# Fourteen tiles of the merge gates between the keys and the delta rule, parked in DRAM, and the recurrence traced ahead of the next projections

## The chip, the cores and the metric

The kernel runs on one core of a Trainium2 chip. The metric is the device time of one execution in microseconds, the median of several runs. The core has TensorE (PE: matmuls, and PEld: its weight loads), VectorE (DVE), ScalarE (ACT), GpSimd (POOL) and the queue engine SyncE (SP), which only issues DMAs here. Each engine carries out its instructions in a fixed order.

## The reference, cut to what matters

One decoder layer over 512 tokens of 1024 channels, in float32. The first sub-layer is a token mixer: one input projection `h @ w_in`, whose columns are shared out among two branches and the merge gates.

```python
h = x * (1 + sc1) + sh1                       # modulation, from c @ w_ada + b_ada
(q_att, c_kv, q_idx, k_idx, w_idx, qkv, a, b, z, gates) = split(h @ w_in)
y_att = dsa_attention(...)                    # top-128 keys a query, chosen by an indexer
y_dn  = gated_deltanet(...)                   # 8 heads, causal conv, delta rule in chunks, gated norm with z
gates = sigmoid(gates);  g_att, g_dn = gates[..., :1024], gates[..., 1024:]
merged = g_att * (y_att @ w_br_att) + g_dn * (y_dn @ w_br_dn)
x = layer_norm(alpha * x + (1 + gt1) * (merged @ w_out))
```

The second sub-layer is a mixture of 32 experts (two for each token), followed by a second layer norm. The gates depend on `h` and `w_in` alone, and are not used before the merge.

## The kernel before, in words

All activations are kept transposed, 128 channels by 512 tokens in a tile. A projection tile (`project`, L274) makes 128 output channels: 8 slices of the inner dimension, and for each slice 3 matmuls, since every float32 operand is split into a high and a low part (`mm3`, L226), so 24 matmuls of 512 columns. Its weights are a 128x1024 piece. Two pieces are loaded together into one of the three buffers "w" (`raw_of`, L242), and each is then split (`split_w`, L213) by ACT (high part, L222) and by VectorE or GpSimd (low part, L223). Which of the two takes the low part is told by the list `lo_eng`: GpSimd at first, VectorE for seven splits from the latent key/value tiles on (L501), then GpSimd again, and VectorE from the merge on (L861). The list `plan` (L232 to L240) holds the order of all weight pieces; `look_ahead` splits the next of them after each projection.

The stages, in order: the modulation of `x`; the small tile and the eight key tiles with their convolutions and norms (`key_norms`); the decays and the triangular matrices of the delta rule, whose 32x32 blocks are inverted on VectorE (L489 to L498) and pass through DRAM; the latent key/value tiles (`T_CKV`), the indexer's queries (`T_QI`) and its scores; the eight heads of the delta rule; eight heads of attention; the merge; the output projection with layer norm and routing; the experts.

A head of the delta rule is written as: transposes, the q.k products, the chain F, FtB, FtW, FtFtW that puts the 128x128 inverse XT together from the blocks in BB, the norm of the head before (`gated`), the next head's query and value projections with their convolutions (`queries_values`), the projection of z (`gate_z`), and then the recurrence over four chunks (L705 to L726: pw, wv, pv, vn, po, pS, St), of which each step needs the one before. After heads 2, 3 and 4 VectorE selects the top keys (`select`, 32 passes each).

The merge runs over eight channel tiles `d`: two gate tiles (`T_G + 2d` and `T_G + 2d + 1`, tanh by ACT into `gth`), two branch tiles, VectorE's products and sum, and the halves of the result. The pieces of the modulation that are needed last (`mod_cols`, L200: load of 1 MB of `w_ada` into a buffer "w", two passes of VectorE and a short one) stand there, three for each of `d` = 1 to 5 and one for `d` = 6.

The program is traced in this order, and a planner then fixes each engine's order: an instruction that was traced earlier goes first among those that its model takes to be ready. So the matmuls of a projection and the steps of a chain lie interleaved on PE. `issue_after` keeps an instruction behind another one. DMAs that `ld` issues are in SP's queue, those of `s.dma_start` in ACT's, those of `g.dma_start` in POOL's.

## Time and profile before

| | |
|---|---|
| median of 3 runs | 1262.67 us (1258.73 to 1264.76) |
| the profiled execution | 1262.51 us, span 1260.5 us |
| PE busy | 1181.4 us, 94% |
| VectorE busy | 786.0 us, 62% |
| ACT busy | 434.2 us, 34% |
| GpSimd busy | 215.8 us, 17% |
| HBM read and written | 287.05 MB, 3.70 MB |

The busy time of an engine is the time in which an instruction of it runs. Matmuls overlap in the array, so a busy PE is not always one at its peak. The granted clock is the share of TensorE's full clock that the chip allowed in a stretch; it has two levels, 2.4 GHz (1.0) and 1.2 GHz (0.5). Idle time before an instruction is put down to what released it.

### The profile page before, as it was taken

The page shows a single profiled execution, that of the slowest core. Times are in us where ns is not written, and L with a number is a line of the kernel's source. Part 1 is how long each engine was busy: PE and PEld are TensorE (multiplying, and loading weights), DVE is VectorE, ACT ScalarE, POOL GpSimd, SP SyncE. Part 2 cuts the span into 40 slices and gives each one's busy share as a digit, 9 for nine tenths or more (in the row PEclk, how much of TensorE's full clock was granted, in tenths as well). Part 3 has the DMA queues.
Part 4 walks back from the last instruction along what each step waited for, and adds up shares of the span by engine and source line. Part 5 has one row for each costly group of instructions (what it writes and reads, how often), then busy time and mean ns, then how long its engine had stood idle before and what let it go on. Part 6 is the DMA issues. An engine that isn't in the chain of part 4 may idle for free. (4 is left out here: it accounts for less than half of the span.)

```text
span 1260.5 us, 16329 instructions
## 1 busy us (share of the span) xinstructions
PE 1181.4 (94%) x6062; PEld 805.4 (64%) x6062; DVE 786.0 (62%) x1709; ACT 434.2 (34%) x916; POOL 215.8 (17%) x181
## 2 busy tenths in 40 slices
PE   4978988998899999999999979999999999999996
PEld 2767766776677777778888866455445555555543
DVE  6797998598996556876745884734444342433256
ACT  3454643665555656432222232121111111111102
POOL 4332334233232321000013331000000000000002
PEclk8999998999999999999999999999999999999997
DMA  7614414221111112266635677779999999999992
GB/s 276 260 67 130 122 43 138 60 44 54 49 66 38 67 54 81 83 252 234 252 132 200 244 300 304 309 291 420 420 421 420 422 421 420 421 421 422 420 381 103
DMA packets 76115, 291.84 MB, mean 232 GB/s; under 512 B 19297, under 2 KB 31745, under 8 KB 51458
## 3 DMA queue, kind: packets, MB, share of 16 engines
q1 hardware_dynamic: 58994, 282.47, 57.2%
q10 hardware_dynamic: 16352, 6.16, 2.1%
q0 software_dynamic: 688, 2.15, 0.5%
q8 instruction: 49, 0.80, 0.3%
q14 instruction: 32, 0.26, 0.1%
HBM read 287.05 MB, written 3.70 MB: 231 GB/s over the span
## 5 line engine op out<-in xcount | busy, mean ns | idle before, releaser
L227 PE MATMUL pj<-h_hi,w_hi 128*128 128x512 f32 (+1 forms) x504 | 202.5, 408 | 15.7 <-ACT h_hi L322 10.8
L229 PE MATMUL pj<-h_hi,w_lo 128*128 128x512 f32 (+1 forms) x504 | 206.1, 410 | 4.7 <-POOL w_lo L223 4.7
L228 PE MATMUL pj<-h_lo,w_hi 128*128 128x512 f32 (+1 forms) x504 | 206.5, 410 | 0.0
L223 POOL TENSOR_TENSOR w_lo<-wr,w_hi 128x1024 fp32r<-128x1024 f32 x43 | 108.8, 2533 | 205.5 <-ACT w_hi L222 163.9
L222 ACT ACTIVATE w_hi<-wr 128x1024 fp32r<-128x1024 f32 x85 | 89.7, 1057 | 133.3 <-PE pj L228 86.7
L227 PEld LDWEIGHTS pj<-h_hi,w_hi 128*128 128x128 f32 x504 | 97.1, 193 | 37.7 <-ACT h_hi L322 13.2
L1270 PE MATMUL pwg<-wg,xg 128*64 128x512 f32 x512 | 115.2, 595 | 0.0
L1270 PE MATMUL pwu<-wu,xg 128*64 128x512 f32 x512 | 115.2, 592 | 0.0
L229 PEld LDWEIGHTS pj<-h_hi,w_lo 128*128 128x128 f32 x504 | 98.1, 195 | 24.2 <-POOL w_lo L223 6.6
L228 PEld LDWEIGHTS pj<-h_lo,w_hi 128*128 128x128 f32 x504 | 97.4, 193 | 18.4 <-DVE h_lo L323 0.8
L1282 PE MATMUL py<-wd,hbTs 128*64 128x512 f32 x480 | 106.3, 593 | 0.0
L1270 PEld LDWEIGHTS pwu<-wu,xg 128*64 128x64 f32 x512 | 46.7, 137 | 62.9 <-issue 60.6
L1194 DVE TENSOR_TENSOR acc<-acc,comb 128x512 f32<-128x512 f32 (+1 forms) x126 | 77.4, 668 | 11.6 <-PE comb L1185 6.6
L1192 POOL TENSOR_TENSOR acc<-acc,ad 128x256 f32<-128x256 f32 x6 | 4.6, 788 | 449.9 <-PE comb L1185 447.0
L1144 DVE SCALAR_TENSOR_TENSOR eth<-eth,pwg 128x512 f32<-128x512 f32 x16 | 11.0, 687 | 112.5 <-ACT eth L1143 112.5
L1282 PEld LDWEIGHTS py<-wd,hbTs 128*64 128x64 f32 x480 | 40.0, 137 | 62.9 <-issue 62.9
L1270 PEld LDWEIGHTS pwg<-wg,xg 128*64 128x64 f32 x512 | 36.8, 137 | 65.3 <-issue 62.2
L223 DVE TENSOR_TENSOR w_lo<-wr,w_hi 128x1024 fp32r<-128x1024 f32 x42 | 55.6, 1325 | 29.1 <-ACT w_hi L222 28.2
L356 DVE SCALAR_TENSOR_TENSOR cacc<-pad,convw,cacc 128x512 f32<-128x512 f32 x72 | 68.5, 956 | 6.2 <-ACT cacc L354 6.1
L1163 DVE SCALAR_TENSOR_TENSOR ys<-py,gsl,gt2r 128x512 f32<-128x512 f32 (+1 forms) x34 | 24.3, 718 | 69.5 <-PE py L1282 62.9
L1146 DVE SCALAR_TENSOR_TENSOR hb<-eth,pwu 128x512 f32<-128x512 f32 x16 | 17.2, 1077 | 74.2 <-PE pwu L1270 74.2
L964 ACT ACTIVATE xg<-gx,h2c 128x256 f32<-128x256 f32 x32 | 17.8, 564 | 127.0 <-PE gx L1206 119.3
(492 smaller groups left out, 2339.9 us busy)
## 6 DMA issues: line engine op xcount, KB each, us to landing
wg<-in_w_gate_dram SPq DMA_DIRECT2D x64, 1024.0 KB, 11.4
wu<-in_w_up_dram SPq DMA_DIRECT2D x64, 1024.0 KB, 15.3
wd<-in_w_down_dram SPq DMA_DIRECT2D x60, 1024.0 KB, 12.4
wr<-in_w_in_dram SPq DMA_DIRECT2D x31, 1024.0 KB, 5.0
wada<-in_w_ada_dram SPq DMA_DIRECT2D x23, 1024.0 KB, 5.4
wr<-in_w_br_dram SPq DMA_DIRECT2D x8, 1024.0 KB, 6.4
gr<-g_rows ACTq DMA_DIRECT2D x16, 256.0 KB, 4.8
wr<-in_w_out_dram SPq DMA_DIRECT2D x4, 1024.0 KB, 5.0
```

Of the source, the lines that this page charges most:

```text
L222: s.activation(hi, raw, AF.Copy)
L223: (lo_eng.pop() if len(lo_eng) > 1 else lo_eng[0]).tensor_tensor(lo, raw, hi.bitcast(F32), op=OP.subtract)
L227: pe.matmul(o, a[0], b[0], start=start, stop=False)
L228: pe.matmul(o, a[0], b[1], start=False, stop=False)
L229: pe.matmul(o, a[1], b[0], start=False, stop=stop)
L356: v.scalar_tensor_tensor(acc, pad[:, i:i + S], convw[:, ct, i:i + 1], acc, op0=OP.mult, op1=OP.add)
L964: x = s.activation(xg[:, j, :n], o[:, 0, :n], AF.Identity, bias=h2c[:, 1, 1, j:j + 1], scale=h2c[:, 1, 0, j:j + 1])
L1146: rows_done[0] = v.scalar_tensor_tensor(hb[:n], th[:n].rearrange("s (p j) -> s j p", j=4), 0.5, pu[:n].rearrange("s (p j) -> s j p", j=4), ...
L1163: v.scalar_tensor_tensor(ys[:n, :w], py, gs, gt2r[:n, c], op0=OP.mult, op1=OP.mult)
L1194: v.tensor_tensor(acc[:, t, c], acc[:, t, c], o[:, :w], op=OP.add)
L1270: done = pe.matmul(o[64 * x:64 * x + 64], xg[:, 4 * i + j, c0 + 64 * x:c0 + 64 * x + 64], ws[x][:, j * FF:(j + 1) * FF], start=(i == 0 and ...
L1282: pe.matmul(py[c][64 * x:64 * x + 64], hT[:, 2 * i + j, 64 * x:64 * x + 64], ws[x][:, j, 512 * c:512 * c + 512], start=(i == 0 and j == 0) ...
```

## The change

Fourteen of the sixteen gate tiles (all but the first and the last) are projected earlier, two at a time: two after the key norms, two after the latent key/value tiles, and two in each of the heads 1 to 5 of the delta rule, behind that head's recurrence and the next head's projections. Each goes through tanh on ACT into a buffer and is written to a DRAM tensor by ACT's queue; in the merge, SP's queue loads it back into `gth`. In each head the recurrence is traced ahead of the next head's query and value projections and of z. Of the sixteen pieces of the modulation, eight are traced in attention, one at the start of each head, and eight in the merge, two for each of `d` = 1 to 4.

```diff
--- before.py
+++ after.py
@@ -41,6 +41,7 @@
 OVER = 16
 ACC_AT = 4
 GATED_AT = 3
+GATES_AT = (1, 2, 3, 4, 5)
 SELECT_AT = (2, 3, 4)
 
 EARLY = ['w', 'w', 'w', 'xa', 'o0', 'o1', 'a0', 'k0', 'k1', 'm0', 'm1', 'm2', 'acc0', 'k2', 'k3', 'm3', 'h0', 'h1', 'acc1']
@@ -228,15 +229,24 @@
         pe.matmul(o, a[0], b[1], start=False, stop=False)
         pe.matmul(o, a[1], b[0], start=False, stop=stop)
 
+    def early_gates(n):
+
+        return [("w_in", T_G + 1 + 2 * n + i) for i in range(2)]
+
     raws, pending = {}, {}
-    plan = [("w_in", i) for i in range(T_QI + 4)]
-    plan += [("w_in", T_QVZ + i) for i in range(3 * H)]
+    plan = [("w_in", i) for i in range(T_CKV)] + early_gates(0)
+    plan += [("w_in", i) for i in range(T_CKV, T_CKV + 2)] + early_gates(1) + [("w_in", i) for i in range(T_QI, T_QI + 4)]
+    plan += [("w_in", T_QVZ + i) for i in range(2)]
+    for h in range(H):
+        plan += [("w_in", T_QVZ + 2 + 3 * h + i) for i in range(3 if h < H - 1 else 1)]
+        plan += early_gates(GATES_AT.index(h) + 2) if h in GATES_AT else []
     for h in range(H):
         if h in (0, 3):
             plan.append(("w_ukv", h // 3 * 2))
         plan.append(("w_in", T_QA + h))
     for d in range(KT):
-        plan += [("w_in", T_G + 2 * d), ("w_in", T_G + 2 * d + 1), ("w_br", 2 * d + 1), ("w_br", 2 * d)]
+        plan += [("w_in", T_G + 2 * d + b) for b in range(2) if not 0 < 2 * d + b < 2 * KT - 1]
+        plan += [("w_br", 2 * d + 1), ("w_br", 2 * d)]
     plan += [("w_out", k) for k in range(2)]
 
     def raw_of(key, pool_=None):
@@ -280,6 +290,16 @@
             mm3(o, (hi[:, k, :], lo[:, k, :]), (r[0][:, k, first:], r[1][:, k, first:]), k == 0, k == KT - 1)
         look_ahead()
         return o
+
+    gate_rows = dram.tile([2 * KT, P, S], F32, name="gate_rows")
+
+    def work_out_gates(n, pool_):
+
+        for _, i in early_gates(n):
+            o = project("w_in", i)
+            x = pool_.tile([P, S], F32, name="gst", bufs=2)
+            s.activation(x, o, AF.Tanh, scale=0.5)
+            s.dma_start(gate_rows[i - T_G], x)
 
     h_hi = Parts(bigtile("h_hi", F32R), bigtile("h_hi", F32R))
     h_lo = Parts(bigtile("h_lo", F32R), bigtile("h_lo", F32R))
@@ -448,6 +468,7 @@
     for h in range(HB, H):
         conv_silu(first.get(T_K + h) or project("w_in", T_K + h), 8 + h, kT[:, h, :])
     key_norms(1)
+    work_out_gates(0, ip)
 
     def decay(h, e=g):
 
@@ -505,6 +526,7 @@
         o = project("w_in", T_CKV + c)
         s.activation(sqc[:, c, :], o, AF.Square)
         v.tensor_scalar(cks[:, c, :], o, kvg[:, c:c + 1], None, op0=OP.mult)
+    work_out_gates(1, ip)
 
     p_ss = pc("p_ss", (P, NT))
     for t in range(NT):
@@ -689,14 +711,8 @@
         xt_done = v.tensor_tensor(XT[:64, :, 64:], XT[:64, :, 64:], four("FtFtW", F[:96, :, :64], FW[:96]), op=OP.add)
         if done:
             gated(*done)
-        if h < H - 1:
-            qv[h + 1] = queries_values(h + 1)
         if h == H - 1:
             late_rows.append(smalltile("ou"))
-        zs = gate_z(h)
-        if h == H - 1:
-            V.append([bigtile("V", F32R) for _ in range(2)])
-            att_values(0)
 
         po = pc("po", (P, NT, P))
         St = None
@@ -729,6 +745,14 @@
         else:
             ou = dq.tile([P, NT, P], F32, name="ou", bufs=1)
         s.activation(ou, po, AF.Copy)
+        if h < H - 1:
+            qv[h + 1] = queries_values(h + 1)
+        zs = gate_z(h)
+        if h == H - 1:
+            V.append([bigtile("V", F32R) for _ in range(2)])
+            att_values(0)
+        if h in GATES_AT:
+            work_out_gates(GATES_AT.index(h) + 2, dq)
         if h in SELECT_AT:
             with tc.issue_after(xt_done.ins):
                 select(1 + SELECT_AT.index(h))
@@ -748,6 +772,7 @@
         if h == 3:
             V.append([tp_.tile([P, NT, S], F32R, name=n) for n in ("V_hi", "V_lo")])
             att_values(1)
+        mod_cols(16 + 2 * h, tp_)
         V_hi, V_lo = V[h // 4]
         look_ahead()
         o = project("w_in", T_QA + h)
@@ -860,16 +885,18 @@
     ys = (Parts(ya_hi, yb[0]), Parts(*ya_lo, yb[1])), (Parts(*yd[0]), Parts(*yd[1]))
     lo_eng[0] = v
     for d in range(KT):
-        for j in range(16 + 6 * (d - 1), min(22 + 6 * (d - 1), 48), 2) if 1 <= d <= 6 else ():
+        for j in (28 + 4 * d, 30 + 4 * d) if 1 <= d <= 4 else ():
             mod_cols(j, ep)
         if d == KT - 2:
             m_rows = mod_rows()
             h2c = first_norm_rows()
         part = [None, None]
         for b in range(2):
-            o = project("w_in", T_G + 2 * d + b)
             part[b] = ep.tile([P, S], F32, name="gth", bufs=4)
-            s.activation(part[b], o, AF.Tanh, scale=0.5)
+            if 0 < 2 * d + b < 2 * KT - 1:
+                ld(part[b], gate_rows[2 * d + b])
+            else:
+                s.activation(part[b], project("w_in", T_G + 2 * d + b), AF.Tanh, scale=0.5)
         for b in (1, 0):
             o = project("w_br", 2 * d + b, rhs=ys[b])
             v.scalar_tensor_tensor(part[b], part[b], 1.0, o, op0=OP.add, op1=OP.mult)
```

## Rows read from the trace of the kernel before

**Rows 1.** Busy time of the engines by stretch; last: granted clock, DMA share, GB/s.
```profile
core 0: us, PE busy (x) PEld busy (x) DVE busy (x) ACT busy (x) POOL busy (x), PEclk, DMA share, GB/s
100.00:225.00 125.00, 110.13 (x555) 90.02 (x555) 104.57 (x224) 63.80 (x141) 43.17 (x54) 0.95 0.37 111
225.00:400.00 175.00, 157.97 (x972) 126.48 (x971) 147.50 (x388) 101.53 (x280) 54.20 (x32) 0.98 0.18 51
100.00:400.00 300.00, 268.10 (x1524) 216.50 (x1524) 252.07 (x611) 165.32 (x421) 97.37 (x86) 0.97 0.26 76
400.00:520.00 120.00, 119.24 (x618) 93.68 (x617) 73.88 (x253) 69.63 (x162) 26.64 (x16) 1.00 0.17 58
523.90:692.10 168.20, 168.20 (x723) 135.26 (x722) 109.42 (x174) 48.02 (x80) 17.99 (x17) 1.00 0.59 213
692.00:1260.00 568.00, 547.18 (x2889) 302.34 (x2887) 268.01 (x520) 102.73 (x178) 37.22 (x24) 0.98 0.90 365
```

**Rows 2.** The same view, 25 us in the heads with a selection.
```profile
350.00:375.00 25.00, 22.06 (x128) 17.62 (x126) 25.00 (x58) 13.21 (x37) 9.01 (x5) 1.00 0.13 43
```

**Rows 3.** PE's waits from 100 to 400 us: total, times, longest.
```profile
PE pw L706 <- DVE St L725: 5.5, 2, 3.8
PE pv L712 <- DVE wv L708: 5.4, 4, 1.8
...
PE pv L712 <- DVE XT L689: 2.3, 2, 1.5
PE vtr L643 <- DVE vT L359: 2.2, 1, 2.2
```

**Rows 4.** Waits of SP's queue from 690 to 900 us.
```profile
SPq L1107 <- PE po L229: 29.9, 6, 13.0
```

**Rows 5.** PE in order of time, about the start of the merge: start, us.
```profile
519.40 0.45 PE L228 MATMUL pj<-h_lo,w_hi 128*128 128x512 f32 x1
...
524.12 0.40 PE L227 MATMUL pj<-yd_hi,w_hi 128*128 128x512 f32 x1
```

**Rows 6.** The page's groups by line: count, busy us, mean ns, idle before.
```profile
L223 POOL TENSOR_TENSOR w_lo<-wr,w_hi 128x1024 fp32r<-128x1024 f32 x43 | 108.8, 2533 | 205.5 <-ACT w_hi L222 163.9
L222 ACT ACTIVATE w_hi<-wr 128x1024 fp32r<-128x1024 f32 x85 | 89.7, 1057 | 133.3 <-PE pj L228 86.7
...
L223 DVE TENSOR_TENSOR w_lo<-wr,w_hi 128x1024 fp32r<-128x1024 f32 x42 | 55.6, 1325 | 29.1 <-ACT w_hi L222 28.2
```

**Rows 7.** Instructions on the tile gth: ns shortest/median/longest, first and last start.
```profile
L880 DVE TENSOR_TENSOR m<-gth,m x32: 271/284/2500, 539.3 to 697.6; 128x128 fp32r<-128x128 f32 x32
L872 ACT ACTIVATE gth<-pj x16: 575/580/598, 520.1 to 681.9; 128x512 f32<-128x512 f32 x16
L875 DVE SCALAR_TENSOR_TENSOR gth<-gth,pj x16: 681/687/689, 530.9 to 692.3; 128x512 f32<-128x512 f32 x16
```

**Rows 8.** The same view of the tile gr.
```profile
L455 ACTq DMA_DIRECT2D gr<-g_rows x16: 366/382/726, 100.0 to 319.9; - x16
```

**Rows 9.** All engines in order of time, about 160 us.
```profile
159.80 0.74 DVE L552 SCALAR_TENSOR_TENSOR isc<-rl,widx,isc 128x512 f32<-128x512 f32 x1
...
160.45 2.63 POOL L223 TENSOR_TENSOR w_lo<-wr,w_hi 128x1024 fp32r<-128x1024 f32 x1 [7.30 <-ACT w_hi L222]
...
160.89 2.74 DVE L552 SCALAR_TENSOR_TENSOR isc<-rl,widx,isc 128x512 f32<-128x512 f32 x1
```

**Rows 10.** VectorE's groups by line from 523 to 692 us.
```profile
L205 DVE SCALAR_TENSOR_TENSOR junk<-wada,cond 128x1024 bf16<-128x1024 f32 x32 | 39.1, 1222 | 6.9 <-DMA wada<-in_w_ada_dram 6.2
...
L207 DVE SCALAR_TENSOR_TENSOR mod<-mod,bada 128x2 f32<-128x2 f32 x16 | 2.5, 157 | 0.3
```

**Rows 11.** The page's DMA issues: count, KB each, us to landing.
```profile
wada<-in_w_ada_dram SPq DMA_DIRECT2D x23, 1024.0 KB, 5.4
wr<-in_w_br_dram SPq DMA_DIRECT2D x8, 1024.0 KB, 6.4
gr<-g_rows ACTq DMA_DIRECT2D x16, 256.0 KB, 4.8
```

## The prediction

> **What bounds the kernel now.** I read the stretches first, because the page's 94% for PE is a mean over stages with different limits. In the merge, from 523.9 to 692.1 us, PE is busy for all 168.2 us [rows 1]: the reader is to see a stage with no hole in it, where the 30 tiles that run there (16 branch tiles, 14 gate tiles, each 24 matmuls) cost 168.2 / 30 = 5.61 us each, and where VectorE has 109.4 us of work and so room. From 100 to 400 us, which holds the end of the key work, the inverses, the index scores and the eight heads of the delta rule, PE is busy for 268.1 of 300 us, a share of 0.894; 31.9 us are idle, and its granted clock averages 0.97, against 1.00 in the merge [rows 1]. A mean of 0.97 over 300 us of the levels 2.4 and 1.2 GHz is 18 us at the lower one, so up to 9 us of PE's busy time there is slowness. VectorE is the other party: 252.1 of 300 us, and 25.00 of 25.00 us between 350 and 375 [rows 1, 2]. The list of waits then says what PE's idle time there is: short waits for VectorE's steps in the recurrence (St 5.5 us, wv 5.4, XT 2.3) and for the next head's values (vT 2.2) [rows 3]. So one stage is filled up by PE, and an earlier one has holes that no work fills, or that PE's fixed order cannot fill.
>
> After the merge DMA is busy for 0.90 of the time [rows 1], and SP's loads of expert weights wait for the products that free their buffers, 29.9 us of it for the output projection [rows 4]. What follows the merge therefore starts from its end, and I let it move as one block.
>
> **The change, part by part.**
> *Gates out of the merge.* After the change 16 branch tiles and the last gate tile stand there: 13 x 5.61 = 72.9 us go. The 14th, the second gate tile, is what PE runs from 519.40 until the first product with yd at 524.12 [rows 5]. Without it that product waits only for the halves of y; it could come at once (4.7 us more) or no earlier (0). I take 3.5, since the halves of eight heads are made one after the other just then. Sum: -76.4 us.
>
> *The same tiles from 100 to 400 us.* 14 x 5.61 = 78.5 us of PE work are added to a stretch with 31.9 us of holes, so its length is (268.1 + 78.5 - c) / u, where c is clock won back and u PE's busy share. The ends: u = 0.894 as now, and u = 119.2 / 120 = 0.994, which attention reaches in the same kernel with the next projection always at hand and VectorE at 73.9 of 120 us [rows 1]. The new stretch lies between: the gate tiles need no VectorE pass after their product, so VectorE's share falls, but PE still carries its instructions in one planned order, and a recurrence step at the head of it that VectorE delivers late stops the gate tile behind it too. I take 0.95, the middle rounded up, since four tiles fall in 100 to 225 us (PE 110.1 of 125) and ten in the heads. For c I take 4.5 of the 9 us (ends 0 and 9), since a denser PE leaves fewer idle spells. (346.6 - 4.5) / 0.95 = 360.1: the stretch grows by 60.1 us.
>
> The Trainium skill, in "Perfetto Trace Analysis", section "Identifying the Most-Contended Engine", holds that matmul busy time is a poor measure of PE's headroom and that the weight loads' busy share is a better one. By the rows that share is 216.5 / 300 = 0.722 here and 135.3 / 168.2 = 0.804 in the merge [rows 1]; with 14 x 135.3 / 30 = 63.1 us added and the merge's share the stretch would last 279.6 / 0.804 = 348 us and the kernel end near 1238. With attention's share, 93.7 / 120 = 0.781, it would last 358 us, close to the sum above.
>
> *What comes with a moved tile.* Each brings its split, on ACT 1.06 us and on POOL 2.53 instead of VectorE's 1.33 in the merge [rows 6], a tanh of 0.58 [rows 7] and a write to DRAM issued by ACT, nearest a row read's 0.38 [rows 8]. ACT gets 14 x (1.06 + 0.58 + 0.38) = 28 us on 165, over 360 us: about 54%, so nothing waits in the mean, and the cover is PE's own 5.6 us a tile. POOL gets 35 us on 97; queued behind a split are the next head's decay, qd and the clearing of BB, which can start up to 2.5 us later a head. The price of a POOL split for VectorE shows at 160.45: while it runs, a pass that took 0.74 us just before takes 2.74 [rows 9]. So 14 more cost VectorE 0 to 14 x 2.0 = 28 us; I take half, 14, with which VectorE is at 266 of 360 us. The mean is no bound, but the heads with a selection are close to one, and this is why u is not nearer to 0.994. SP gets no issue here beyond loads that it had later.
>
> *The recurrence ahead of the next projections.* The matmuls that this reorders all remain. At best the recurrence's three waits (5.5 + 5.4 + 2.3 = 13.2 us) go [rows 3]; at worst the next head's values come late every time, 7 x 2.2 = 15.4 us. PE already runs the two interleaved, so I take 0 beyond u.
>
> *Columns of the modulation in attention.* Eight of the sixteen pieces move there, each two passes of 1.222 us and one of 0.157 [rows 10]: 2.60 us, 20.8 in all on VectorE, 94.7 of 120 us. SP issues one load of 1 MB a head ahead of the next query tile's; three buffers hold it, the keys' weights and the query pair. PE's filler covers it; without cover, one pass late in each head, 8 x 1.22 = 9.8 us. I take +1.
>
> *The merge's new pace.* A channel tile lasts PE 2 x 5.61 = 11.2 us instead of 22.4. VectorE's work for one of tiles 1 to 4 is two splits (2 x 1.33), two products and a sum (3 x 0.69), four halves (4 x 0.28) [rows 6, 7] and two pieces (2 x 2.60): 11.1 us, level with PE. The loads are one branch pair and two pieces through three buffers: 6.4 + 5.4 + 5.4 = 17.2 us from issue to landing if each waited for the one before [rows 11], 6.0 too many in each of four tiles, 24 us; 0 if they overlap. SP also issues the 14 reads of parked gates, 256 KB each, for which 4.8 us is the nearest row [rows 11]; such a read waits for one of four buffers, and the next weight pair is queued behind it, but two channel tiles of lead cover that. I take +3.
>
> Sum: -76.4 + 60.1 + 1 + 3 = -12.3 us on the profiled execution's 1262.5 (span 1260.5 and 2.0 around it), so 1250. The median of the three runs is 1262.7, so no correction is needed.
>
> **The rivals.**
> *The holes all fill.* With u = 0.994 and the full 9 us of clock the stretch lasts 337.6 / 0.994 = 339.6, +39.6 us; with no stall elsewhere -36.8, so 1226. For it: gate tiles depend on nothing of the heads, and attention shows the share. Against it: VectorE's full slices and PE's short waits, which are not for lack of a filler alone. Chance 0.20.
>
> *PE's share does not rise.* Place: the heads with a selection. Price: 346.6 / 0.894 = 387.7, +87.7 us; with the rest -76.4 + 87.7 + 4 = +15.3, so 1278. It decides from a share below 342.1 / (300 + 72.4) = 0.919, where the stretch takes all that the merge gives. For it: every wait in the list is for VectorE or ACT, which get later when POOL splits more. Against it: a head that waits for VectorE is just where a free tile can run. Chance 0.13. The Trainium skill, in "SBUF — State Buffer", section "Who interferes with whom", speaks for this rival: a VectorE instruction with two SBUF inputs and a GpSimd one that reads SBUF exclude each other for a whole instruction. The trace agrees at 160.89 (2.74 for 0.74 us); by it all 14 splits would cost their whole 2.53 us, 35 us instead of 14.
>
> *The merge waits for its weights.* If three buffers make the loads follow one another, the merge pays 24 us and not 3: +8.7, so 1271. For it: the pace doubles while two pieces a tile remain. Against it: the pieces are not needed before the seventh tile and can slip into the tiles that have none. Chance 0.09.
>
> **How the numbers follow.** The forecast has 0.58, with an own range of 1239 (u = 0.97, no stall elsewhere) to 1258 (u = 0.93). The measurement tells 0.5%, 6.3 us, from no change: faster is below 1256.2, slower above 1268.8. Faster: 0.45 of the forecast's 0.58, most of its own range lying below 1256, and the 0.20 of filled holes, 0.65. Within: the rest of the forecast, 0.13. Slower: 0.13 + 0.09 = 0.22. The range goes from 1228, just above the end where all is filled, to 1272, past the weights' case.
>
> **What would show it.** Right: the stretch from the first product with yd to the output projection near 95 us after 168; the stretch up to attention about 60 us longer, PE at 0.95; POOL splits between 100 and 460 us 14 more; attention within 2 us. Wrong: PE's share there at 0.92 or less, or 0.98; holes of PE in the merge that end with a load or a VectorE split; VectorE busy above 290 us in the stretch; the expert phase not moved with the merge.

## The result: 2.3% slower, and the profile after

The changed kernel takes 1292.2 us (median of four runs, 1290.8 to 1295.7) where the kernel before took 1263.7 beside it: a ratio of 1.0234, with a 95% interval from 1.0207 to 1.0261. The forecast was 1250 us and its range ended at 1272. The profiled span is 1289.0 us, 28.5 us longer than before.

I cut both traces at the same events, because the borders of [rows 1] fall elsewhere in the changed kernel: the copy `ou` of the last head (end of the delta rule), the last copy of `oT` (end of attention) and the first product of the output projection (end of the merge).

| stretch | before | after | change | forecast |
|---|---|---|---|---|
| 100 us to the last `ou` copy | 314.4 | 393.9 | +79.5 | +60.1 |
| attention | 105.8 | 132.9 | +27.1 | +1 |
| merge | 172.0 | 98.7 | -73.3 | -76.4 + 3 |
| the rest | 568.3 | 563.6 | -4.7 | 0 |

The merge did what was forecast, to a tenth of a microsecond. The two stretches that had to take in what left it cost 45.5 us more than forecast. Here are the windows of the kernel after that answer to [rows 1] (columns as there); the first two are the part up to the first head's `ou` copy and the heads, the last is what follows the merge.

```profile
100.00:256.40 156.40, 131.41 (x682) 107.88 (x681) 114.56 (x245) 76.10 (x176) 42.97 (x57) 0.93 0.32 97
256.40:493.90 237.50, 224.63 (x1256) 177.73 (x1254) 163.75 (x398) 119.06 (x293) 84.32 (x45) 1.00 0.26 82
100.00:493.90 393.90, 356.04 (x1934) 285.60 (x1934) 278.31 (x642) 195.16 (x468) 127.29 (x101) 0.97 0.28 87
493.90:626.80 132.90, 117.85 (x560) 93.98 (x559) 98.61 (x272) 64.00 (x152) 28.15 (x16) 0.94 0.33 116
626.80:725.50 98.70, 95.47 (x407) 75.58 (x407) 76.09 (x126) 28.61 (x55) 18.11 (x17) 1.00 0.68 239
725.50:1289.00 563.50, 541.75 (x2888) 298.88 (x2886) 267.94 (x520) 102.67 (x178) 38.48 (x24) 0.99 0.90 367
```

The same borders in the kernel before:

```profile
100.00:239.20 139.20, 122.86 (x645) 100.60 (x645) 112.00 (x243) 71.32 (x169) 45.44 (x56) 0.95 0.34 101
239.20:414.40 175.20, 159.39 (x959) 126.90 (x957) 146.59 (x389) 100.91 (x268) 56.56 (x32) 0.98 0.19 53
100.00:414.40 314.40, 282.25 (x1602) 227.49 (x1601) 258.58 (x631) 172.23 (x436) 102.00 (x88) 0.97 0.25 74
414.40:520.20 105.80, 105.29 (x541) 82.85 (x540) 67.37 (x231) 62.92 (x150) 22.00 (x15) 1.00 0.18 60
```

The reader is to see three things. First, from 100 us to the end of the heads PE's share is 356.04 / 393.9 = 0.904; it was 0.898, the forecast needed 0.95, and below 0.919 the stretch takes all that the merge gives. Read as lengths: PE's busy time grew by 356.04 - 282.25 = 73.8 us, and its idle time did not shrink but grew, from 314.4 - 282.25 = 32.2 us to 37.9. On balance no hole was filled. Second, the two parts of that stretch differ. The heads did reach 0.946, and their idle time fell from 15.8 to 12.9 us; in the part before them the share fell from 0.883 to 0.840, the idle time rose from 16.3 to 25.0 us, and the granted clock fell from 0.95 to 0.93. Third, attention, where PE had been busy for 105.29 of 105.8 us, now has 15 us of holes and a clock of 0.94.

PE's waits in the kernel after say what ends those holes (in us: total, times, longest). First those from 100 to 494 us, then those of attention; in attention the kernel before has one wait, of 0.2 us.

```profile
PE pv L728 <- DVE wv L724: 8.8, 6, 1.9
PE pidx L566 <- ACT rl L569: 8.3, 4, 4.3
PE kk L496 <- DVE NTm L498: 7.5, 3, 5.6
PE vtr L665 <- DVE vT L379: 2.6, 1, 2.6
...
```

```profile
PE pt L815 <- DVE pr L812: 6.7, 4, 2.3
PE sc L229 <- DVE K_lo L797: 3.1, 1, 3.1
PE sc L229 <- DVE qk L797: 3.0, 1, 3.0
PE oT L228 <- ACT T_hi L816: 1.0, 2, 0.8
...
```

The waits for `NTm` (matrices of the delta rule) and for `rl` (index scores) stand in the part before the first `ou` copy. They were there before, about half as long; [rows 3] shows the lines around them:

```profile
PE kk L475 <- DVE NTm L477: 4.2, 2, 2.1
PE pidx L544 <- ACT rl L547: 3.4, 2, 1.8
```

That part holds one long chain: the products `kk`, the matrices `NTm`, their way through DRAM, the inversion of the blocks on VectorE, and the way back through `r_dram` to the first head. Here are the first of the inversion's two lines and the write behind it, in the kernel before and after (ns shortest/median/longest, first and last start in us):

```profile
L493 DVE TENSOR_TENSOR y<-y,y x31: 184/348/422, 146.1 to 207.8; 128x31 f32<-128x31 f32 x2, 128x60 f32<-128x60 f32 x2, 128x87 f32<-128x87 f32 x2, 128x112 f32<-128x112 f32 x2
...
L498 POOL DMA_DIRECT2D r_dram<-y x1: 577/577/577, 210.3 to 210.3; - x1
```

```profile
L514 DVE TENSOR_TENSOR y<-y,y x31: 180/357/2374, 158.9 to 218.8; 128x31 f32<-128x31 f32 x2, 128x60 f32<-128x60 f32 x2, 128x87 f32<-128x87 f32 x2, 128x112 f32<-128x112 f32 x2
...
L519 POOL DMA_DIRECT2D r_dram<-y x1: 577/577/577, 223.3 to 223.3; - x1
```

From the start of the inversion to the write it takes 64 us in both kernels. It starts 12.8 us later, and the write comes 13.0 us later: the chain was pushed back as a whole, and work that PE does ahead of it fills none of its holes. In ten_heads, which lacks the four gate tiles of this part, the inversion starts at 146.9 us and the write at 211.9.

`K_lo`, `qk` and `pr` are steps of attention's own chain on VectorE. Why they are late is seen in the kernel after in order of time at 549 us (start, us; in brackets the engine's idle time before it):

```profile
549.08 9.79 SPq L203 DMA_DIRECT2D wada<-in_w_ada_dram  x2
...
553.93 1.23 DVE L206 SCALAR_TENSOR_TENSOR junk<-wada,cond 128x1024 bf16<-128x1024 f32 x1 [5.77 <-DMA wada<-in_w_ada_dram]
...
554.19 3.20 POOL L224 TENSOR_TENSOR w_lo<-wr,w_hi 128x1024 fp32r<-128x1024 f32 x1 [5.13 <-ACT w_hi L223]
...
554.80 0.59 ACT L796 ACTIVATE K_hi<-pK 128x512 fp32r<-128x512 f32 x1
...
555.20 3.27 DVE L206 SCALAR_TENSOR_TENSOR junk<-wada,cond 128x1024 bf16<-128x1024 f32 x1
...
559.00 0.68 DVE L797 TENSOR_TENSOR K_lo<-pK,K_hi 128x512 fp32r<-128x512 f32 x1
```

VectorE stands idle for 5.77 us because the next pass in its order, a pass of the modulation, waits for its weights; then the first pass takes 1.23 us, the second, beside a GpSimd split, 3.27. `K_lo`, whose input `K_hi` was there at 554.80 + 0.59 = 555.4, starts at 559.00, and PE waits 3.1 us for it. Over the whole of attention, VectorE's groups by line (busy us, mean ns | idle before):

```profile
L206 DVE SCALAR_TENSOR_TENSOR junk<-wada,cond 128x1024 bf16<-128x1024 f32 x16 | 24.1, 1506 | 5.8 <-DMA wada<-in_w_ada_dram 5.8
...
L208 DVE SCALAR_TENSOR_TENSOR mod<-mod,bada 128x2 f32<-128x2 f32 x8 | 6.3, 787 | 0.0
```

So the pieces take 30.4 us there instead of the 20.8 of the forecast. The load is late once only; the smallest of a piece's three operations, 157 ns in the merge [rows 10], averages 787 and costs more. Five of its eight runs take 141 to 152 ns. The other three take 1.65 to 2.27 us, and each lies beside a GpSimd split, as here:

```profile
530.00 2.37 POOL L224 TENSOR_TENSOR w_lo<-wr,w_hi 128x1024 fp32r<-128x1024 f32 x1 [10.50 <-ACT w_hi L223]
...
530.12 2.27 DVE L208 SCALAR_TENSOR_TENSOR mod<-mod,bada 128x2 f32<-128x2 f32 x1
...
533.48 0.30 PE L815 MATMUL pt<-ident,pr 128*128 128x128 f32 x1 [2.28 <-DVE pr L812]
```

Behind each of the three, `pr` comes late and PE waits for it: 2.0, 2.3 and 1.6 us of the 6.7 in the list. The page's line of the splits answers to [rows 6]: of the 85 splits GpSimd now has 57, 14 more, and VectorE 14 fewer, since the gates' splits in the merge had been its own.

```profile
L224 POOL TENSOR_TENSOR w_lo<-wr,w_hi 128x1024 fp32r<-128x1024 f32 x57 | 141.9, 2490 | 297.1 <-ACT w_hi L223 241.9
```

### The profile page after: what moved, and what is told of

Read it like the earlier page. It is cut to its first block, busy times and chain, and to the rows that moved or that the text cites. A ratio compares the mean times of both kernels' runs of the same rounds, so it can differ in the third digit from the quotient of the medians.

```text
span 1289.0 us, 16416 instructions
## 1 busy us (share of the span) xinstructions
PE 1184.0 (92%) x6062; PEld 807.7 (63%) x6062; DVE 798.3 (62%) x1695; ACT 433.8 (34%) x916; POOL 250.4 (19%) x195
## 5 line engine op out<-in xcount | busy, mean ns | idle before, releaser
L228 PE MATMUL pj<-h_hi,w_hi 128*128 128x512 f32 (+1 forms) x504 | 204.9, 413 | 14.9 <-ACT h_hi L342 13.0
L224 POOL TENSOR_TENSOR w_lo<-wr,w_hi 128x1024 fp32r<-128x1024 f32 x57 | 141.9, 2490 | 297.1 <-ACT w_hi L223 241.9
L376 DVE SCALAR_TENSOR_TENSOR cacc<-pad,convw,cacc 128x512 f32<-128x512 f32 x72 | 77.0, 1074 | 8.4 <-ACT cacc L374 8.3
L991 ACT ACTIVATE xg<-gx,h2c 128x256 f32<-128x256 f32 x32 | 17.8, 564 | 127.0 <-PE gx L1233 119.3
L1212 PE MATMUL comb<-yh,places 128*128 128x512 f32 (+1 forms) x132 | 53.0, 405 | 0.5 <-ACT eth L1261 0.5
## 6 DMA issues: line engine op xcount, KB each, us to landing
wg<-in_w_gate_dram SPq DMA_DIRECT2D x64, 1024.0 KB, 11.3
wd<-in_w_down_dram SPq DMA_DIRECT2D x60, 1024.0 KB, 12.3
gr<-g_rows ACTq DMA_DIRECT2D x16, 256.0 KB, 5.1
```

Source lines behind the costliest of these rows:

```text
L224: (lo_eng.pop() if len(lo_eng) > 1 else lo_eng[0]).tensor_tensor(lo, raw, hi.bitcast(F32), op=OP.subtract)
L228: pe.matmul(o, a[0], b[0], start=start, stop=False)
L376: v.scalar_tensor_tensor(acc, pad[:, i:i + S], convw[:, ct, i:i + 1], acc, op0=OP.mult, op1=OP.add)
L991: x = s.activation(xg[:, j, :n], o[:, 0, :n], AF.Identity, bias=h2c[:, 1, 1, j:j + 1], scale=h2c[:, 1, 0, j:j + 1])
L1212: pe.matmul(o[:, :w], OT[:n, t * P:(t + 1) * P], y, start=(i == 0), stop=(not bias and i == len(parts) - 1))
```

## The experiments

Every kernel was timed in turn with the kernel before; ratios are to it, with 95% intervals. The table has the lengths in us of the four stretches named above in each profiled execution, and the start of the first `ou` copy; the sections follow it. Each length is that of one execution. What follows the merge is the same work in every run and yet lies between 563.6 and 575.1 us, so differences of a few us in a stretch are not to be leaned on.

| run | first ou | 100 to last ou | attention | merge | rest | ratio |
|---|---|---|---|---|---|---|
| before | 239.2 | 314.4 | 105.8 | 172.0 | 568.3 | 1 |
| after | 256.4 | 393.9 | 132.9 | 98.7 | 563.6 | 1.0234 |
| mod_alone | 243.0 | 319.5 | 115.4 | 171.3 | 569.0 | 1.0077 |
| rec_alone | 244.2 | 317.0 | 113.6 | 171.9 | 570.6 | 1.0056 |
| gates_alone | 259.5 | 408.9 | 107.2 | 116.6 | 570.6 | 1.0269 |
| mod_back | 256.1 | 395.4 | 111.2 | 112.8 | 570.0 | 1.0177 |
| gates_before_rec | 253.6 | 395.8 | 111.2 | 113.1 | 570.8 | 1.0201 |
| one_slice | 248.2 | 347.4 | 111.2 | 113.9 | 569.0 | 0.9865 |
| no_products | 239.8 | 311.3 | 111.4 | 111.9 | 566.2 | 0.9523 |
| four_early | 256.0 | 360.1 | 107.3 | 161.8 | 570.4 | 1.0274 |
| four_slice | 251.1 | 339.7 | 107.3 | 161.5 | 566.4 | 1.0072 |
| four_early_dve | 254.6 | 346.8 | 107.0 | 162.9 | 571.3 | 1.0172 |
| split_on_dve | 253.3 | 380.5 | 111.2 | 114.8 | 572.5 | 1.0092 |
| ten_heads | 244.1 | 359.6 | 111.2 | 119.3 | 570.4 | 1.0005 |
| ten_heads_dve | 241.2 | 353.9 | 111.2 | 120.7 | 575.1 | 0.9970 |
| spread14_dve | 230.2 | 374.7 | 114.2 | 112.1 | 568.5 | 1.0092 |
| ten_dve_norec | 240.8 | 356.7 | 107.2 | 118.8 | 571.2 | 0.9968 |

### One part of the change alone

mod_alone puts only the eight pieces of the modulation into attention, on the kernel before:

```diff
+        mod_cols(16 + 2 * h, tp_)                       # at the start of each head of attention
-        for j in range(16 + 6 * (d - 1), min(22 + 6 * (d - 1), 48), 2) if 1 <= d <= 6 else ():
+        for j in (28 + 4 * d, 30 + 4 * d) if 1 <= d <= 4 else ():
```

> The kernel before, with only the eight pieces of the modulation moved into attention. In the changed kernel the time from the last head's ou to the last oT copy grew from 105 to 132 us. Theory (the pieces' VectorE passes and their loads' waits stand in the softmax chain): attention about 125 to 132 us here too, the merge no shorter since PE fills it, the whole 1280 to 1290. Rival (attention grew since its filler, the gate tiles, is gone or since the selections slipped): attention within 3 us of 105, the whole 1261 to 1267.

Measured: 1273.2 us, 1.0077 [1.0055, 1.0099]. Attention is 9.6 us longer and the merge, which PE fills, is not shorter (-0.7). That lies between the two readings. PE's waits in attention add up to 6.2 us here against 14.9 in the kernel after; none of the eight sums of two columns is held (the longest takes 472 ns). The pieces alone are a small loss.

rec_alone traces only the recurrence ahead of the next head's projections (the block that calls `queries_values`, `gate_z` and `att_values` moves behind the `ou` copy).

> The kernel before, with only the recurrence traced ahead of the next projections. Theory (this reorders work that PE interleaves anyway): first to last ou within 6 us of the 175 before, the whole 1258 to 1270. Rival (this order makes the heads wait, and is what took the holes' filling away): first to last ou 185 to 200 us, the whole 1274 to 1289.

Measured: 1270.7 us, 1.0056 [1.0036, 1.0076]. The heads, from the first to the last `ou` copy, are 2.4 us shorter; the first `ou` copy comes 5.0 later and attention is 7.8 longer. Part of the 7.8 is the border: the last head's z and attention's first values now stand behind the `ou` copy that ends the heads, so 556 products lie in attention instead of 541, some 3.5 us at 5.61 / 24 each. The 5.0 go with the granted clock, which up to the first `ou` copy is 0.92 here and 0.95 in the kernel before.

gates_alone takes the fourteen gates out of the merge and leaves recurrence and pieces as before; mod_back is the kernel after with the sixteen pieces back in the merge (the diff of mod_alone the other way round).

> The kernel before, with only the fourteen gate tiles moved (the sixteen pieces of the modulation stay in the merge, the recurrence stays behind the projections). Theory (the gate tiles run as blocks between the heads, not in the holes): first ou at 255 and first to last ou 230 to 240 us, attention near 105, the merge a little longer than in the changed kernel because five tiles carry three pieces at 11.2 us; the whole 1268 to 1282. Rival (the recurrence order spoilt the filling): first to last ou 205 to 220 us, the whole 1240 to 1256.

> The changed kernel with the eight pieces of the modulation back in the merge. Theory (pieces in attention cost 27 us): attention near 105 us, the merge 8 to 15 us longer than 99, the whole 1270 to 1282. Rival (attention's growth has another cause): attention stays at 125 or more, the whole 1290 to 1305.

Measured: gates_alone 1300.4 us, 1.0269 [1.0205, 1.0333]; mod_back 1288.5 us, 1.0177 [1.0131, 1.0223]. Read as a ladder: the gates alone lengthen the stretch up to the last `ou` copy by 94.5 us and shorten the merge by 55.4; the recurrence ahead then gives 13.5 us back in that stretch and takes 4.0 in attention; the pieces in attention cost 21.7 us there and give the merge 14.1. So the recurrence ahead, a loss of 7 us by itself, is worth 12 us with the gates in the heads by the medians, though the two intervals overlap; the 4.0 us in attention are the border again (559 products for 538). The place of the pieces hardly moves the whole: the profiled spans are 1289.0 us after and 1289.3 in mod_back, and the intervals overlap. Both kernels came out slower than expected (1282 at most). PE's waits in the merge of mod_back show why the pieces matter there now:

```profile
PE pj L228 <- ACT w_hi L223: 6.2, 3, 2.8
PE pj L230 <- DVE w_lo L224: 5.3, 6, 1.6
PE pj L229 <- DVE yd_lo L768: 1.6, 3, 0.9
```

With the gates gone the merge is no longer full: PE is busy for 99.3 of 112.8 us, and what it waits for are splits, of weights and of the halves. One of the waits for `w_hi` goes back to a load. SP can issue it only when VectorE is through with a piece (661.37), ACT stands idle until it lands, and PE waits 2.27 us:

```profile
661.37 0.38 SPq L262 DMA_DIRECT2D wr<-in_w_br_dram  x1
...
669.10 1.06 ACT L223 ACTIVATE w_hi<-wr 128x1024 fp32r<-128x1024 f32 x1 [11.42 <-DMA wr<-in_w_br_dram]
...
670.21 0.51 PE L228 MATMUL pj<-yd_hi,w_hi 128*128 128x512 f32 x1 [2.27 <-ACT w_hi L223]
```

The forecast's 3 us for this merge holds with half of the pieces away, not with all sixteen in it.

gates_before_rec is mod_back with a head's two gate tiles traced and planned ahead of its recurrence and not behind it.

> The changed kernel with the pieces in the merge, in which a head's two gate tiles are traced and planned right after XT and ahead of the recurrence, so that they can lie in the chain's holes instead of behind the recurrence. Theory (PE is full in these heads, and its remaining idle time is waits in a fixed order): first to last ou 232 to 246 us, the whole 1281 to 1296. Rival (the tiles ran as a block behind the chain, and its holes stayed empty for that): first to last ou 215 to 228 us, the whole 1264 to 1278.

Measured: 1289.4 us, 1.0201 [1.0165, 1.0237]; every stretch within 0.8 us of mod_back's, save the first `ou` copy, 2.5 us earlier. Whether a head's two tiles are planned ahead of its recurrence or behind it makes no difference that shows.

### What of a tile costs: its products, or what comes with it

one_slice and no_products are mod_back with less in each gate tile, so they compute less than the kernel does and serve only to split up its time.

```diff
-            o = project("w_in", i)
+            o = project("w_in", i, slices=1)            # one_slice: 3 of 24 matmuls
+            s.activation(x, h_hi[:, (i - T_G) % KT, :]...)  # no_products: no weights, no split, no product
```

> The changed kernel with the pieces of the modulation in the merge, in which the fourteen gate tiles take only the first of eight slices of the inner dimension (3 of 24 matmuls), with splits, tanh, writes and reads as they were. Theory (PE's own time of the tiles is the price in the heads): first to last ou 175 to 195 us instead of 239, the whole 1215 to 1245. Rival (the splits on GpSimd and what they hold up are the price): first to last ou 215 us or more, the whole above 1262.

> The changed kernel with the pieces in the merge, in which the fourteen gate tiles have no weights and no products at all: the tanh of a slice of h is written to DRAM in their places and read back in the merge. Theory (the loads, splits and products are all of the price): last ou at 405 to 424 us against 495 with them and 447 with one slice, the whole 1190 to 1212. Rival (the recurrence's place and the writes cost the heads time): last ou at 435 or more, the whole above 1222.

Measured: 0.9865 [0.983, 0.9901] and 0.9523 [0.9497, 0.9549]. With no_products the last `ou` copy comes 3 us earlier than before: parking the rows, the tanh and the recurrence ahead cost nothing there. With one slice the heads (199.2 us) and the whole (1246.3) lie just above the ranges of its first reading.

From no_products to one_slice the stretch grows by 36.1 us, for 14 x 3 matmuls that are worth 14 x 5.61 / 8 = 9.8 us, so 26 us come beside the products. From one_slice to mod_back it grows by 48.0 us for the other 294 matmuls, 68.7 us of work at the merge's pace, so 20.7 us are missing. It is tempting to read the 26 us as an entry fee of loads and splits, and the 20.7 as products that ran in the holes. The rows of the stretch (no_products, one_slice, mod_back) speak against it:

```profile
100.00:411.30 311.30, 279.94 (x1598) 224.56 (x1598) 258.60 (x631) 176.58 (x444) 98.45 (x87) 0.97 0.27 83
...
100.00:447.40 347.40, 302.23 (x1657) 240.35 (x1658) 264.56 (x646) 192.55 (x464) 126.70 (x101) 0.94 0.31 98
...
100.00:495.40 395.40, 358.17 (x1944) 287.75 (x1942) 276.63 (x641) 195.30 (x469) 127.26 (x101) 0.97 0.28 87
```

PE's idle time is 31.4, 45.2 and 37.2 us. The granted clock is 0.97, 0.94 and 0.97, which, reckoned as in the prediction, is some 9, 21 and 12 us of work lost at the lower level. So of the 26 us, 13.8 are new holes and some 12 are clock, which one_slice has and the full kernel has not; and of the 20.7 us, 8.0 go into holes that only one_slice has, some 9 are clock that comes back, and some 4 are left without a place. From the first row to the last, 78.5 us of products add 78.2 us to PE's busy time and 5.9 us to its idle time. The tiles cost their whole length, and a little more.

### The four early tiles

four_early moves only the gates of the first section, on the kernel before; four_slice is the same with 3 of 24 matmuls; four_early_dve the same with all products, and the four splits on VectorE.

```diff
-GATES_AT = (1, 2, 3, 4, 5)
+GATES_AT = ()
-            if 0 < 2 * d + b < 2 * KT - 1:
+            if 0 < 2 * d + b < 5:
```

> The kernel before, with only the first four gate tiles moved (two after the key norms, two after the latent key/value tiles); ten stay in the merge, the rest is as before. Theory (from 100 us to the first head a chain through g_rows, the decays, the inverses and r_dram sets the pace, and the four tiles push its start back instead of filling holes): first ou at 252 to 260 us instead of 239, the merge 22 us shorter, the whole 1254 to 1266. Rival (the delay of the first head comes from the head tiles behind): first ou at 239 to 246, the whole 1243 to 1252.

> The kernel before with the four early gate tiles, of which only one of eight slices is multiplied (12 matmuls in place of 96). Theory (loads, splits and the order of the tiles push the later projections back, not PE's time): last ou at 430 to 448 us against 460 with all slices and 414 without the tiles, the whole 1260 to 1282. Rival (PE's time of the four is the price): last ou at 412 to 422, the whole 1240 to 1250.

> The four early tiles alone, on the kernel before, their splits on VectorE and not on GpSimd. Against the same with splits on GpSimd (first ou copy 256.0, last 460.1, whole 1299.6 us). If GpSimd's splits are over half of what the four tiles cost, the last ou copy comes at 435 to 445 and the whole is about 1280. If it is their place in the order of tiles, the last ou copy stays at 455 to 460 and the whole within 5 us of 1299; if VectorE's inverse (146.7 to 208.8 in the kernel before) is what the splits then delay, the first ou copy comes after 260 us.

Measured: 1.0274 [1.0235, 1.0313], 1.0072 [1.0042, 1.0102] and 1.0172 [1.0129, 1.0215]. Four tiles, 22.4 us of products, push the last `ou` copy back by 45.7 us, and the merge gives only 10.2 (PE waits there once for 5.6 us, for a split whose weights are loaded late). The first `ou` copy comes at 256.0 us, where the theory of the pushed chain had it; the whole, 1299.6 us, is 34 us above that theory's range, which had no loss in the heads and the full 22 us in the merge. With an eighth of the products the stretch is still 25.3 us longer. The rows of the stretch, four_early and four_early_dve:

```profile
100.00:460.10 360.10, 315.15 (x1710) 254.06 (x1709) 271.75 (x640) 180.66 (x449) 105.56 (x92) 0.94 0.25 74
...
100.00:446.80 346.80, 308.36 (x1712) 250.15 (x1711) 267.61 (x636) 179.57 (x445) 101.00 (x89) 0.96 0.26 80
```

Against the kernel before, the 45.7 us are 12.8 of idle time (45.0 for 32.2) and 32.9 of busy time, of which 22.4 are the products and some 12 the clock: 0.94 of 360.1 us against 0.97 of 314.4. The clock is as low with an eighth of the products. The splits on VectorE take 13.3 us off, less than a third of the 45.7 and not the half that the theory of the splits asked for; about half of the 13.3 is clock and half idle time. The first `ou` copy hardly moves (254.6): it is felt in the heads (192.2 us for 204.1).

### Splits on VectorE, ten tiles, and the place of the four

split_on_dve is mod_back with the splits of the fourteen gate tiles on VectorE; ten_heads is mod_back without the four early tiles (their gates stay in the merge); ten_heads_dve has both.

```diff
+                                       eng=v if plan[0][0] == "w_in" and T_G < plan[0][1] < T_G + 15 else None)
-    work_out_gates(0, ip)
-    work_out_gates(1, ip)
```

> The changed kernel with the pieces in the merge, in which the low parts of the fourteen gate tiles are made by VectorE (1.2 us) instead of GpSimd (2.5 us). Theory (PE's time is the price): within 6 us of the 1288.5 with GpSimd. Rival (GpSimd's splits hold VectorE up and with it the chains): first to last ou 225 to 232 us, the whole 1270 to 1281.

> The changed kernel with the pieces in the merge and without its four early tiles: only the ten gate tiles in the heads 1 to 5 are moved, behind the recurrence that is traced ahead. Theory (the four early tiles cost 46 us up to the last head since all that follows them in the tiles' order comes later; the ten cost less than their own 56 us of PE): first ou at 238 to 246, last ou at 446 to 462 us, the whole 1244 to 1262. Rival (a moved tile costs its own length or more wherever it stands): last ou at 470 or more, the whole above 1266.

> The same ten tiles, their low parts made by VectorE. Theory (GpSimd's splits hold up VectorE and stand ahead of the heads' own GpSimd work): last ou 5 to 14 us earlier than with GpSimd, the whole 1236 to 1254. Rival (what the fourteen gained by this came from the early four alone): within 4 us of ten_heads.

Measured: split_on_dve 1276.0 us, 1.0092 [1.0055, 1.0128]; ten_heads 1263.3, 1.0005 [0.9977, 1.0034]; ten_heads_dve 1262.0, 0.997 [0.9943, 0.9996]. Fourteen splits moved to the other engine are worth 12.5 us of the whole by the medians and 14.9 us before the last `ou` copy, although VectorE takes on passes of 1.22 us for them. The costliest pass of the heads on VectorE shows what a split does there, first in mod_back, then in split_on_dve, last in the kernel before (mean ns after the comma):

```profile
L376 DVE SCALAR_TENSOR_TENSOR cacc<-pad,convw,cacc 128x512 f32<-128x512 f32 x30 | 38.7, 1290 | 3.7 <-ACT cacc L374 3.7
```

```profile
L377 DVE SCALAR_TENSOR_TENSOR cacc<-pad,convw,cacc 128x512 f32<-128x512 f32 x30 | 31.0, 1032 | 1.9 <-ACT cacc L375 1.8
...
L224 DVE TENSOR_TENSOR w_lo<-wr,w_hi 128x1024 fp32r<-128x1024 f32 x8 | 9.8, 1219 | 3.1 <-ACT w_hi L223 2.7
```

```profile
L356 DVE SCALAR_TENSOR_TENSOR cacc<-pad,convw,cacc 128x512 f32<-128x512 f32 x24 | 19.7, 822 | 0.0
```

The same pass over as much data takes 1290 ns in heads with 29 GpSimd splits, 1032 with 19, and 822 in the kernel before, with 16. It is a matter of which passes meet a split: in mod_back the 15 of 30 that overlap one average 1.84 us and the other 15 average 0.74; in split_on_dve 9 of 30 overlap one, in the kernel before 3 of 24. Thirty of them make 7.7 us, which pays for most of the 9.8 us of splits that VectorE takes on. The row of the stretch in split_on_dve, against mod_back's row above, says where the 14.9 us are:

```profile
100.00:480.50 380.50, 349.25 (x1932) 280.49 (x1931) 274.75 (x646) 194.69 (x465) 99.30 (x88) 0.99 0.30 93
```

VectorE's busy time is nearly the same (276.63 and 274.75 us). PE's idle time is 6.0 us less, and its busy time 8.9 us less, with the clock at 0.99 for 0.97, some 8 us. With ten tiles the engine of the splits matters little (ten_heads and ten_heads_dve overlap).

spread14_dve is split_on_dve with the four early tiles moved to heads 0 and 6, so two stand behind each of heads 0 to 6. ten_dve_norec is ten_heads_dve with the recurrence behind the projections, as before.

```diff
-GATES_AT = (1, 2, 3, 4, 5)
+GATES_AT = (0, 1, 2, 3, 4, 5, 6)                        # spread14_dve, early_gates from 0 on
```

> All fourteen gate tiles inside the heads, two behind each of heads 0 to 6, none in the first section; their splits on VectorE, the pieces of the modulation in the merge. It differs from the run with the splits on VectorE (last ou copy 480.5 us, span 1278.9) in the place of four tiles alone. Theory PLACE (the four early tiles cost more than their products because they stand ahead of the tiles that feed the first heads): a tile inside the heads cost (453.9 - 411.3) / 10 = 4.3 us in the run of ten tiles on VectorE, so the last ou copy comes at 453.9 + 4 x 4.3 = 471, the merge is 22 us shorter than there, and the whole is 1260.8 + 17 - 22 = 1256 us. Theory SIDE (each tile costs the same wherever it stands: loads, splits, order): the last ou copy stays at 480 and the whole at 1276 to 1279. Between: 1267.

> The ten gate tiles of the heads, splits on VectorE, with the recurrence behind the projections as in the kernel before. If the recurrence ahead is worth with ten tiles what it was with fourteen (1300.4 against 1288.5), the whole is 1262 + 12 = 1274 us, with the loss in the heads. If it costs what it cost alone (+7), the whole is 1255 us: 5 us earlier at the first ou copy or in attention, and faster than the kernel before by 0.6%.

Measured: spread14_dve 1274.9 us, 1.0092 [1.0055, 1.0128], the same ratio as split_on_dve; ten_dve_norec 1259.8, 0.9968 [0.9944, 0.9991]. The theory that the four tiles are dear by their place holds in part: out of the first section they bring the first `ou` copy to 230.2 us, 23 us earlier, but the last one only 5.8 earlier where it asked for 9.5, attention takes 3.0 back, and the whole stays near where the other theory had it. And ten tiles do not need the recurrence ahead: without it the stretch is 2.8 us longer and attention 4.0 shorter, which is about the border's shift (543 products in attention for 564). Of the kernels that do all the work, ten_dve_norec and ten_heads_dve have the best times, 0.3% under the kernel before and so within the 0.5% that the prediction counts as no change.

Four more tiles (ten_heads_dve to spread14_dve) cost 20.8 us before the last `ou` copy and 3.0 in attention and give the merge 8.6, not 22.4. Past ten tiles the price is near that of the products and the return is not: the merge by then waits for splits (11.3 us of idle time for 3.8) and its clock is 0.97 for 1.00.

## Why the prediction was wrong

**What bounds the kernel: right.** The merge before was full, and it fell by what its tiles cost.

**Gates out of the merge, -76.4, and its new pace, +3: right as a sum** (-73.3 measured), with PE busy for 95.47 of 98.70 us and 3.2 us of waits. Two things had to hold for it together: in mod_back, with all sixteen pieces there, the same merge shrinks by 59.2 only. The step that had the pieces "slip into the tiles that have none" held for eight.

**The stretch from 100 us, +60.1: the step that failed is PE's share of 0.95.** It stands for holes that take up products: of 31.9 us idle, 360.1 - 342.1 = 18.0 were to be left. The idle time is 37.9 us, so the holes account for the whole miss of 19.4 us. PE's busy time grew by 73.8 us, and the forecast had 78.5 - 4.5 = 74.0; that is luck in part, since the clock, from which the 4.5 were to come, is 0.97 in both kernels.

In the part before the first `ou` copy the idle time grew by 8.7 us. The four tiles there were counted as filler of a stage with holes; they stand ahead of a chain of which VectorE's inversion is the longest link, and push it back by 12.8 us. Without them (ten_heads) the chain starts as before and the idle time of that part is 16.9 us instead of 24.2 (mod_back). The prediction took its waits from the recurrence and passed over those for `NTm` and `rl`, the ones that grew. It also says that every wait in the list is for VectorE or ACT; one, of 2.0 us, is for a GpSimd split.

In the heads the ten tiles took up only 2.9 us of idle time. PE's waits there are still for the recurrence (`wv`, 8.8 us for 5.4), and planning the tiles ahead of it changes nothing (gates_before_rec). What does change it is the engine of the splits: with the fourteen splits on VectorE the heads' idle time is 9.6 us instead of 13.0 in mod_back, and the stretch 14.9 us shorter. The forecast had 14 us for these splits, but as busy time of VectorE (266 of 360 us, so not the bound), with nothing added to the end. That the two figures are close is chance: VectorE's busy time does not fall when the splits move. What it comes to is idle time and clock of PE. By which passes it gets there was not followed further than `cacc`. With the tiles spread over the heads as well (spread14_dve) the stretch is 60.3 us longer than before, the forecast's figure, but with 26.6 us idle and not 18.0, so this is no proof of the sum's parts.

The Trainium skill, in "SBUF — State Buffer", section "Who interferes with whom", has a VectorE instruction with two SBUF inputs and a GpSimd one that reads SBUF exclude each other for a whole instruction. The trace agrees with the exclusion: 3.27 us for a pass of 1.23 beside a split, 2.27 us for a sum of 0.15, and 1.84 us for a `cacc` pass of 0.74. The forecast took half of what such a hold would cost if every split met a pass.

**The recurrence ahead, 0: wrong in both directions.** Alone it costs 7 us; with the gates it gives 12 by the medians (gates_alone against mod_back). That attention is 7.8 and 4.0 us longer in these runs is for the most part products that slid across the border, 15 and 21 of them. Why it helps beside the gates and costs without them was not taken apart.

**The pieces in attention, +1 with a bound of 9.8: the second step that failed**, by 20.7 us (21.7 between mod_back and after). The bound took one pass of 1.22 us late in each head. It missed what is queued behind the pass on VectorE: the whole softmax chain stands in order behind it. A late load stops it (once, 5.77 us idle at 548 us), and so does a pass or a sum beside a GpSimd split (passes of 3.36 and 3.27 us, sums of 1.65 to 2.27 three times). Then PE waits, 14.9 us in all, and with the waits its granted clock falls from 1.00 to 0.94: of 132.9 us some 16 are at the lower level of 1.2 GHz, which is 8 us of work lost. The 19 matmuls that slid across the border (560 for 541) are another 4 us. That makes 27, the whole growth. VectorE's work was put into a stage whose PE was full only because VectorE was always in time. For the total it matters less than it looks: left in the merge, the same eight pieces make that stage 14.1 us longer, and mod_back ends where the kernel after does.

**What follows the merge** was 4.7 us shorter, where 0 was forecast. This is the clock of the two executions: the products take 541.75 us for 547.18 [rows 1], at 0.99 for 0.98. In sum: 19.4 us missing in the stretch, 26.1 in attention, 4.7 gained behind, 40.8 us in all between -12.3 and +28.5.

**The rivals.** *PE's share does not rise* is what happened in effect: 0.904 is under its point of decision, 0.919. Its reason was half right: GpSimd's splits do make VectorE later; but the place is not the heads with a selection, since the heads together reached 0.946, and the time also needed attention's loss. Of the prediction's own signs of being wrong, PE's share of 0.92 or less came true, and VectorE above 290 us did not (278.31). *The holes all fill* is refuted by the idle time, 37.9 us. *The merge waits for its weights* did not happen in the kernel after; in mod_back, with all sixteen pieces in the merge, one wait of 2.3 us goes back to a load, and the others end with splits.

The Trainium skill, in "Perfetto Trace Analysis", section "Identifying the Most-Contended Engine", takes the weight loads' busy share for the measure of PE's headroom; by it the prediction's estimate was an end near 1238 us. The share is 285.60 / 393.9 = 0.725 after and was 0.722 in [rows 1]: it did not see that the stretch would fill none of its holes.

**Still open.** Why the heads keep 12.9 us of idle time with ten free tiles beside them: the waits are known, the reason why no tile runs in them is not. Why the four early tiles cost 45.7 us alone and 35.8 on top of ten (ten_heads to mod_back) is in good part clock: some 12 us of work lost beyond the kernel before in the first case, and some 5 beyond ten_heads in the second (0.97 of 395.4 us for 0.98 of 359.6); what keeps the clock low in the first is not shown. Why the sums of the pieces meet GpSimd's splits in the kernel after and not in mod_alone was not separated.

## What to carry to other kernels

Before work is moved from a full stage into the holes of another, ask what sets the length of the other. Where it is a chain on another engine, work ahead of it pushes the chain back and fills nothing; the first link's start tells (here 12.8 us later, the same 64 us long). Then check the result in lengths and not in shares: busy time that grew, idle time that should have shrunk, and the granted clock. A run with an eighth of the products is a poor measure of what comes with a tile, since it has a lower clock and holes of its own (26 us here, where the full kernel shows 6 us more idle time). Count an instruction of a helper engine that holds up another against that engine's chain, not against its mean load. And do not queue a pass that waits for a DMA, or that can be held, ahead of a chain that a full engine depends on: in an in-order queue it delays everything behind it.

## What the runs showed of the hardware that was not expected

Beside a GpSimd split a VectorE pass can last more than twice its time: 1.23 and 3.27 us for two `junk` passes that follow each other. A tiny instruction can be held as long as a large one: the sum of two columns takes 0.14 to 0.15 us in five of eight cases in attention and 1.65 to 2.27 us in the three beside a split. A stage with PE 99% busy (105.29 of 105.8 us, clock 1.00) had a granted clock of 0.94 over 132.9 us once it held 14.9 us of waits; its four longest waits, 2.0 to 3.1 us, are where the clock fell. And fewer products can mean a slower PE: with an eighth of the gate tiles' products the stretch from 100 us had 0.94, with all or none of them 0.97.
